# V weights in another pool, double-buffered keys, gates at urgent priority, and the fill split around the scores

## The chip, the cores and the metric

The kernel runs on one core of a Trainium2 chip. The metric is the device time of one execution in microseconds (us), as a median over runs. A profile is one execution of the same program, recorded by the hardware profiler.

## The reference, cut to what matters

One layer of a streaming encoder is applied to a prompt of 1024 tokens and to 64 further tokens of a running stream (1088 columns in all, model width 1024). One input projection of x feeds two branches:

```python
qa, ka, va, za, qkv_b, a_b, b_b, z_b, g_a, g_b = in_projection(x, w_in)
# A: 16 query heads on 4 key heads of 64, chunks of 64 see their own and two chunks before, a sink in the softmax
qa, ka = partial_rope(qa), partial_rope(ka)
oa  = window_attention(qa, ka, va, attn_sinks)
y_a = (oa * silu(za)) @ w_o_attn
# B: causal convolution, SiLU, normalised q and k, a delta rule in chunks of 64 with decays from a_b, b_b
y_b = (rmsnorm(delta(silu(conv(qkv_b)), gates(a_b, b_b))) * silu(z_b)) @ w_o_delta
h   = sigmoid(g_a) * y_a + sigmoid(g_b) * y_b
y   = layer_norm(ALPHA * x + h @ w_out)
```

Outputs are y, the new keys and values of the window, the last rows before the convolution, and the delta states.

## The kernel before, in words

Tile writes the semaphores. Each instruction has a priority, and a list scheduler with a model of the times decides, before the run, the order of the instructions on every engine and in the DMA queue of SyncE (SP). On the chip each engine then takes its instructions strictly in that order. `urgent()` gives what it encloses the highest priority. Matmuls are kept in the order in which the program traces them (`mm`, L108), transposes too (`tr`, L111), and a `split` with `pin=True` stays behind the ScalarE instruction traced before it.

Every product in full precision is three matmuls: both operands are split into a high and a low part by `split` (L88 on ScalarE, L91 on VectorE), and high*high, high*low and low*high are summed in PSUM. PSUM has eight banks here: three under the tag `pj` (`pjt()`) and five under `bg` (`ps()`).

The program goes through these stages:

1. `load_x` loads and splits x. `branch_a_keys` projects the keys in six groups (three column groups, two pairs of heads). Each group is copied to SBUF (`rraw`), rotated with a shuffled copy (`rsh`), added, split by `key_parts` into `rsh` (high) and `klo` (low), and written to DRAM (`k_d`) by four DMAs for each call of `put`. All of these tiles have one buffer. The last column group calls `put` twice, and the cached keys add two more calls.
2. `vab` projects V and the decay inputs with weights of 272 columns (tile `wt`, both parts and all eight blocks, in pool `vb`). 24 matmuls make one of nine tiles.
3. `plain` weaves `gates` (decays of branch B; its scratch tile is one more tile of tag `klo`) with `early`, the first two tiles of z_A. `early` keeps its tanh results in the tags `rraw` and `rsh`. Two matmul groups of `gates` stand in the order of TensorE: one after the first 24 matmuls of `early`, one after the next 24. The sums of x for the next stage (`sums_x`, GpSimd) follow; their splits are pinned on ScalarE.
4. `front` and `stream` make queries, z_A and merge gates by a seven-product scheme on quarters. Weights come from `weights7` in the tags `whi`, `wlo` and `wx` (three buffers, pool `ws`). The evacuation of a gate is `land` (L407: PSUM plus a saved part into a tile `gs`, urgent), a tanh (L619) and for z_A a multiply (L621) into another `gs`, and a DMA. `gs` has five buffers.
5. `attention` goes through 36 units. Iteration i does `values` of unit i-3, `flip` (transposes the probabilities of unit i-2 into two `bg` banks, copied out by ScalarE and VectorE, L719), `scores` of unit i (eight matmuls into two `bg` banks, L686 to L701 behind them), and then yields `UNIT`. `weave` fills that yield with matmuls of the merge gates until 8797 columns are done. `values` holds two more `bg` banks over two units, until L763 reads them.
6. Branch B: four pairs of heads, projections woven with the delta rule. `pair_project`, `gate_project` and `zb_project` use tiles `gt` (three buffers).
7. `out_a`, `out_b`, `final`: output projections, also with `gt`, and the layer norm. `out_a` loads a stored merge gate into `gt` (L1123), multiplies it with PSUM (L1124), and stores it (L1125). Its first tile evacuates all three column groups at its end.

Of the kernel before, what the change touches and what calls it, by code (L numbers as in the profile page):

```python
# [25 lines left out]
KT = 8  # L26
# [22 lines left out]
UNIT = 8797  # L49
# [6 lines left out]
class Build:  # L56
# [180 lines left out]
    def consts(self):  # L237
        nc, I = self.nc, self.I
        cf = self.t(self.cp, [128, 2 * 128 + 2 * 64], "cf")
        nc.sync.dma_start(cf, I["cf"])  # L240
        c = lambda i: cf[:, i * 128 : (i + 1) * 128]
        self.ident, self.stru2 = c(0), c(1)
        self.later = self.t(self.cp, [128, 128], "later", F32R)
        nc.scalar.activation(self.later, self.stru2, AF.Copy)
        c = lambda i: cf[:, 256 + i * 64 : 256 + (i + 1) * 64]
        self.cmask, self.id64 = (c(i) for i in range(2))
        self.masks = self.t(self.cp, [128, 2, 32], "masks", U8)
        mf = self.t(self.vb, [128, 384], "rsh", bufs=1)[:, :64].rearrange("p (a b) -> p a b", a=2)
        nc.sync.dma_start(mf, I["masks"])
        nc.vector.tensor_copy(self.masks, mf)  # L250
        sm = self.t(self.cp, [128, 24 * 4 + 24 * 3 + 4 + 4 + 1 + 8 + 12], "sm")
        nc.sync.dma_start(sm, I["small"])
        self.convw = sm[:, 0:96].rearrange("p (t j) -> p t j", j=4)
        self.sconv = sm[:, 96:168].rearrange("p (t j) -> p t j", j=3)
        self.alog, self.dtb, self.dnw = sm[:, 168:172], sm[:, 172:176], sm[:, 176:177]
        self.sink = sm[:, 177:185].rearrange("p (g u) -> p g u", u=2)
        self.m4, self.m16, self.m32, self.m64 = sm[:, 185:189], sm[:, 189:191], sm[:, 191:195], sm[:, 195:197]
        self.nsink = self.t(self.cp, [128, 4, 2], "nsink")
        nc.vector.tensor_scalar(self.nsink, self.sink, -1.0, None, ALU.mult)
        self.ncv = self.t(self.cp, [128, 24, 2, 3], "ncv")  # L260
        self.cg = []
        for i in range(2):
            c = self.t(self.ws, [128, HN], "u", bufs=6)[:, :256]
            nc.sync.dma_start(c, I["cg"][:, i * 256 : i * 256 + 256])
            self.cg += [c[:, :128], c[:, 128:]]
# [143 lines left out]

    def vab(self):  # L410
        nc, I = self.nc, self.I
        wt = self.t(self.vb, [128, 2, KT, 272], "wt", F32R)
        hi, lo = wt[:, 0], wt[:, 1]
        for k in (0, 4):
            wr = self.t(self.wp, [128, 4, 272], "wraw", bufs=2)
            with self.urgent():
                nc.sync.dma_start(wr, I["w_vab"][k : k + 4].rearrange("k p c -> p k c"))
                self.split(hi[:, k : k + 4], lo[:, k : k + 4], wr)
        self.V = self.t(self.ap, [128, 9, 256], "V")
        abt = self.t(self.ap, [128, 9, 16], "abt")  # L420
        with self.urgent():
            rest = self.rest(self.t(self.wp, [128, KT, 128], "whi", F32R, bufs=2), self.ring)
        nc.vector.memset(abt, 0.0)
        for t in range(9):
            m = 128 if t < 8 else 64
            ps = self.pjt()
            o = ps[:m, :272]
            for kt in range(KT):
                if t < 8:
                    xh, xl = (self.ring[kt][:, s, t * 128 : t * 128 + m] for s in (0, 1))  # L430
                    self.mm(o, xh, hi[:, kt], kt == 0, False)
                    self.mm(o, xl, hi[:, kt], False, False)
                    self.mm(o, xh, lo[:, kt], False, kt == KT - 1)
                else:
                    self.mm(ps[:, :272], rest[:, kt], hi[:, kt], kt == 0, False)
                    self.mm(ps[:, :272], rest[:, kt], lo[:, kt], False, kt == KT - 1)
            with self.urgent():
                nc.scalar.activation(self.V[:m, t, :], ps[:m, :256], AF.Copy)
                nc.scalar.activation(abt[:m, t, :], ps[:m, 256:272], AF.Copy)
        with self.urgent():  # L440
            for dst, c in ((self.V, slice(0, 256)), (abt, slice(256, 272))):
                nc.vector.tensor_tensor(dst[:m, 8, :], ps[64:128, c], dst[:m, 8, :], ALU.add)
        return abt
# [13 lines left out]
    def early(self):  # L457
        nc = self.nc
        for t in range(2):
            def ev(g, a, n, ps):  # L460
                th = self.t(self.vb, [128, 384], ("rraw", "rsh")[g % 2], bufs=1)[:, :n]
                nc.scalar.activation(th, ps, AF.Tanh, scale=0.5)
                nc.vector.scalar_tensor_tensor(th, th, 1.0, ps, ALU.add, ALU.mult)
                nc.sync.dma_start(self.zA[t, :, a : a + n], th)

            yield from self.project(ev, soon=True)


    def gates(self, abt):
# [3 lines left out]
        sw = self.ps()  # L473
        self.mm(sw[:, :144], swap, abt.rearrange("p t c -> p (t c)"))
        sw = sw[:, :144].rearrange("p (t c) -> p t c", c=16)
        scr = self.t(self.vb, [128, 384], "klo", bufs=1)
        gb = scr[:, 0:144].rearrange("p (t c) -> p t c", c=8)
        g4 = gb.rearrange("p (t two) c -> p t two c", two=2)
        nc.vector.tensor_copy(g4[0:64, :, 0, :], abt[0:64, :, 0:8])
# [51 lines left out]
    def branch_a_keys(self):  # L531
        nc, I = self.nc, self.I
        self.load_rope(self.vb, "rope")


        def put(gp, src, dst):
            n = src.shape[-1]
            for s, part in enumerate(self.key_parts(src)):
                for hf in range(2):
                    nc.sync.dma_start(self.k_d[gp, :, 2 * s + hf, dst : dst + n], part[HS[hf]].bitcast(F32))  # L540

        for g, (a, n) in enumerate(GROUPS):
            for gp in range(2):
                ps = self.ps()[:, :n]
                for kt in range(KT):
                    self.drain(self.mm3(ps, *self.w0[gp], kt, a, n, kt == 0, kt == KT - 1))
                raw, sh = (self.t(self.vb, [128, 384], x, bufs=1)[:, :n] for x in ("rraw", "rsh"))
                nc.scalar.activation(raw, ps, AF.Copy)
                self.rope(raw, sh, a, n, KSWAPMASK)
                nc.vector.tensor_tensor(raw, raw, sh, ALU.add)  # L550
                w = min(n, SEQ - a)
                put(gp, raw[:, :w], a)
                if g == 2:
                    put(gp, raw[:, w:], SEQ + 128)
                    nc.sync.dma_start(self.O["o_nkp"][:, gp], raw[:, w - 128 : w])
                    nc.sync.dma_start(self.O["o_nks"][:, gp, 64:128], raw[:, w:])
        ck = self.t(self.vb, [128, 384], "rraw", bufs=1)[:, :256].rearrange("p (g n) -> p g n", g=2)
        nc.sync.dma_start(ck, I["cache_k"])
        for gp in range(2):
            put(gp, ck[:, gp], SEQ)  # L560
        nc.sync.dma_start(self.O["o_nks"][:, :, 0:64], ck[:, :, 64:128])

    def key_parts(self, src):
        n = src.shape[-1]
        parts = [self.t(self.vb, [128, 384], x, F32R, bufs=1)[:, :n] for x in ("rsh", "klo")]
        self.split(*parts, src)
        return parts

# [9 lines left out]
    def front(self):  # L578
# [32 lines left out]
        def gate(dst, t, silu):  # L611
            def ev(m, a, ps, add):
# [2 lines left out]
                    src = self.t(self.gsp, [128, HN], "gs", bufs=5)  # L615
                    self.land(src, ps, add)
                th = self.t(self.gsp, [128, HN], "gs", bufs=5)
                with nullcontext() if src is not ps else self.urgent():
                    nc.scalar.activation(th, src, AF.Tanh, scale=0.5)  # L619
                    if silu:  # L620
                        nc.vector.scalar_tensor_tensor(th, th, 1.0, src, ALU.add, ALU.mult)  # L621
# [21 lines left out]
    def gate_project(self, tiles):  # L643
        nc = self.nc
        for i in tiles:
            dst = (self.gA, self.gB)[i // 8]

            def ev(g, a, n, ps):
                th = self.t(self.mp, [128, 384], "gt", bufs=3)
                nc.scalar.activation(th[:, :n], ps, AF.Tanh, scale=0.5)  # L650
                nc.sync.dma_start(dst[i % 8, :, a : a + n], th[:, :n])

# [90 lines left out]
    def attention(self):  # L743
# [6 lines left out]
        for i in range(len(units) + 3):  # L750
# [14 lines left out]
            if 1 < i <= len(units) + 1:  # L765
                unit = units[i - 2]
                PT[unit] = self.flip(unit[0], P.pop(unit))
            if i < len(units):
                P[units[i]] = self.scores(*units[i])
            yield UNIT  # L770


    def pair_project(self, p, qkv):
        nc = self.nc
        self.order = LATER if p == 0 else EARLY
        for s in range(3):
            for h in range(2):
# [3 lines left out]
                def ev(g, a, n, ps, s=s, h=h, ct=ct, prev=prev):  # L781
# [13 lines left out]
                        nc.gpsimd.tensor_copy(self.ncv[:, ct, 0, :], pre[:, 256:259])  # L795
                        nc.gpsimd.tensor_copy(self.ncv[:, ct, 1, :], pre[:, 323:326])
                    acc = self.t(self.bp, [128, 384], "acc", bufs=2)
                    th = self.t(self.mp, [128, 384], "gt", bufs=3)
                    cw = lambda j: self.convw[:, ct, j : j + 1]
                    nc.scalar.activation(acc[:, :w], pre[:, 0:w], AF.Copy, scale=cw(0))  # L800
                    for j in range(1, 4):
# [15 lines left out]
    def zb_project(self, p):  # L817
        nc = self.nc
        for h in range(2):
            def ev(g, a, n, ps):  # L820
                th = self.t(self.mp, [128, 384], "gt", bufs=3)
                nc.scalar.activation(th[:, :n], ps, AF.Tanh, scale=0.5)
                nc.vector.scalar_tensor_tensor(th[:, :n], th[:, :n], 1.0, ps, ALU.add, ALU.mult)  # L823
                nc.sync.dma_start(self.zsd[2 * p + h, :, a : a + n], th[:, :n])
# [293 lines left out]
    def out_a(self, w):  # L1118
        nc = self.nc
        for t in range(8):  # L1120
            def ev(g, a, n, ps):
                tg = self.t(self.mp, [128, 384], "gt", bufs=3)
                nc.sync.dma_start(tg[:, :n], self.gA[t, :, a : a + n])  # L1123
                nc.vector.scalar_tensor_tensor(tg[:, :n], tg[:, :n], 1.0, ps, ALU.add, ALU.mult)  # L1124
                nc.sync.dma_start(self.hA[t, :, a : a + n], tg[:, :n])  # L1125
# [2 lines left out]
    def out_b(self, w):  # L1128
# [2 lines left out]
        self.wo = self.t(self.pl, [128, KT, D], "pl", F32R), self.t(self.fp, [128, KT, D], "wolo", F32R)  # L1131
        for t in range(8):
            def ev(g, a, n, ps):
                tg = self.t(self.mp, [128, 384], "gt", bufs=3)
                ha = self.t(self.fp, [128, 384], "ha", bufs=2)
                nc.sync.dma_start(ha[:, :n], self.hA[t, :, a : a + n])
                nc.sync.dma_start(tg[:, :n], self.gB[t, :, a : a + n])
# [301 lines left out]
```

## Time and profile before

| | |
|---|---|
| runs, median (range) | 1448.79 us (1445.99 to 1452.46), 3 runs |
| profiled execution, device time | 1446.86 us |
| its span | 1445.1 us, 30842 instructions |
| TensorE matmul busy | 1375.4 us (95%) |
| TensorE weight load busy | 1280.2 us (89%) |
| VectorE busy | 988.8 us (68%) |
| ScalarE busy | 626.6 us (43%) |
| GpSimd busy | 228.8 us (16%) |
| mean granted clock of TensorE | 0.981 |

The span goes from the first to the last instruction of the profile; the device time has a little around it. PE is the matmul part of TensorE and PEld its weight loads; DVE is VectorE, ACT ScalarE, POOL GpSimd and SP SyncE, whose queue issues nearly all DMAs. "idle before" is time in which an engine had nothing running, and the releaser is what ended it. In a timeline a row gives the start, the length, the line, the operation, the tile written and the tiles read, and in brackets the idle time before it with its releaser. A tile's name is that of its tag, so the scratch tile of `gates` appears as klo.

### The profile page before, as it was taken

The numbers are of one execution on the slowest core, as the hardware profiler recorded it, in microseconds if no ns is written. First come the engines' busy times: TensorE is split into PE (matmuls) and PEld (weight loads), VectorE is DVE, ScalarE is ACT, GpSimd is POOL, SyncE is SP. The second block draws the span as 40 slices with busy tenths as digits, with TensorE's granted clock in tenths as the row PEclk, the third lists the DMA queues.
The fourth block names the chain that finished last, engine by engine and source line by source line (L and its number), as shares of the span: only waits on it lengthen the run. The fifth ranks groups of instructions, "written<-read, shape, count | busy, mean of one in ns | idle before, by whom it ended". The sixth has DMA issues, their size and how long they took to land. (4 is left out here: it accounts for less than half of the span.)

```text
span 1445.1 us, 30842 instructions
## 1 busy us (share of the span) xinstructions
PE 1375.4 (95%) x11850; PEld 1280.2 (89%) x11850; DVE 988.8 (68%) x2404; ACT 626.6 (43%) x1764; POOL 228.8 (16%) x373
## 2 busy tenths in 40 slices
PE   8839999989999999999999999999998999999997
PEld 8839999978888999998899888988898889999886
DVE  7447755656777747977778677867879555654676
ACT  5234444445545535436652565345644344322100
POOL 5114322210011101311130111211130100000000
PEclk9969999999999999999999999999999999999999
DMA  7312576566655541020122102211156224574221
GB/s 262 89 43 75 152 161 166 162 180 165 162 162 153 158 128 45 30 76 16 42 90 88 36 31 66 89 56 46 50 182 199 91 76 141 186 236 153 92 88 73
DMA packets 153013, 162.47 MB, mean 112 GB/s; under 512 B 54305, under 2 KB 136609, under 8 KB 152481
## 3 DMA queue, kind: packets, MB, share of 16 engines
q1 hardware_dynamic: 139664, 150.26, 34.9%
q10 hardware_dynamic: 13200, 10.23, 2.3%
q8 instruction: 94, 1.54, 0.5%
q14 instruction: 55, 0.44, 0.1%
HBM read 111.74 MB, written 48.70 MB: 111 GB/s over the span
## 5 line engine op out<-in xcount | busy, mean ns | idle before, releaser
L108 PE MATMUL pj<-ring,whi 128*128 128x384 f32 (+2 forms) x2856 | 678.5, 328 | 4.2 <-DVE gt L1124 4.2
L108 PEld LDWEIGHTS pj<-ring,whi 128*128 128x128 f32 x2856 | 482.4, 190 | 15.0 <-issue 13.7
L108 PE MATMUL pj<-ring,wlo 128*128 128x384 f32 (+2 forms) x1680 | 464.9, 321 | 0.2
L108 PEld LDWEIGHTS pj<-ring,wlo 128*128 128x128 f32 x1680 | 288.9, 189 | 4.9 <-issue 4.0
L802 DVE SCALAR_TENSOR_TENSOR acc<-pre,sm,acc 128x384 f32<-128x384 f32 (+1 forms) x216 | 134.0, 627 | 26.3 <-ACT acc L800 22.9
L108 PE MATMUL pj<-ring,wx 128*128 128x272 f32 x756 | 109.4, 294 | 10.5 <-DVE gs L407 5.6
L108 PEld LDWEIGHTS pj<-ring,wx 128*128 128x128 f32 x756 | 101.3, 193 | 12.1 <-DVE gs L407 5.8
L88 ACT ACTIVATE whi<-wraw 128x1024 fp32r<-128x1024 f32 (+2 forms) x72 | 66.7, 927 | 79.3 <-PE pj L108 42.6
L91 DVE TENSOR_TENSOR wlo<-wraw,whi 128x1024 fp32r<-128x1024 f32 (+2 forms) x58 | 66.7, 1150 | 38.8 <-ACT whi L88 34.0
L108 PE MATMUL bg<-ring,whi 128*128 128x384 f32 (+2 forms) x408 | 84.7, 318 | 4.3 <-ACT ring L88 4.3
L695 ACT ACTIVATE P<-bg,nm 128x192 f32<-128x192 f32 (+2 forms) x136 | 54.7, 410 | 47.3 <-DVE nm L688 46.1
L108 PEld LDWEIGHTS bg<-ring,whi 128*128 128x128 f32 x408 | 66.1, 192 | 5.8 <-ACT ring L88 4.8
L108 PE MATMUL pj<-pl,ring 128*128 128x512 f32 (+1 forms) x240 | 70.1, 375 | 0.0
L1014 DVE SCALAR_TENSOR_TENSOR S<-S,dec,bg 128x128 f32<-128x128 f32 x128 | 38.7, 344 | 39.1 <-PE bg L108 38.2
L108 PE MATMUL bg<-ring,wlo 128*128 128x272 f32 (+2 forms) x288 | 63.7, 308 | 0.0
L803 ACT ACTIVATE gt<-acc 128x384 f32<-128x384 f32 (+1 forms) x72 | 36.4, 505 | 62.5 <-DVE acc L802 62.2
L992 ACT ACTIVATE qs<-bg,egs 64x128 f32<-64x128 f32 x128 | 46.4, 362 | 29.4 <-DVE R L989 27.6
L330 POOL TENSOR_TENSOR sums<-wraw 128x512 f32<-128x512 f32 x14 | 19.0, 1357 | 243.5 <-DMA wraw<-w_tiles 181.8
L989 DVE SCALAR_TENSOR_TENSOR R<-bg,negc,t2k 64x128 f32<-64x128 f32 x128 | 44.6, 349 | 16.3 <-PE bg L108 15.1
L809 DVE SCALAR_TENSOR_TENSOR plb<-gt,acc 128x384 f32<-128x384 f32 (+1 forms) x96 | 43.1, 461 | 15.6 <-ACT gt L803 15.3
L108 PEld LDWEIGHTS pj<-pl,ring 128*128 128x128 f32 x240 | 44.1, 188 | 8.1
L108 PE MATMUL bg<-keys,q 128*128 128x192 f32 (+2 forms) x272 | 44.2, 289 | 7.3 <-ACT PT L719 3.0
(270 smaller groups left out, 2304.5 us busy)
## 6 DMA issues: line engine op xcount, KB each, us to landing
wraw<-w_tiles SPq DMA_DIRECT2D x80, 512.0 KB, 3.9
q_d<-qsp SPq DMA_DIRECT2D x32, 256.0 KB, 3.5
keys<-k_d SPq DMA_DIRECT2D x28, 256.0 KB, 4.2
q<-q_d SPq DMA_DIRECT2D x64, 96.0 KB, 3.0
gA_d<-gs SPq DMA_DIRECT2D x32, 136.0 KB, 2.6
plb<-prodA SPq DMA_DIRECT2D x8, 544.0 KB, 4.5
plb<-prodB SPq DMA_DIRECT2D x8, 544.0 KB, 4.8
z<-zA_d SPq DMA_DIRECT2D x16, 256.0 KB, 3.1
```

The costliest lines, as they stand in the source:

```text
L88: i = self.nc.scalar.activation(hi, raw, AF.Copy)
L91: self.nc.vector.tensor_tensor(lo, raw, hi.bitcast(F32), ALU.subtract)
L108: self.tc.keep_in_program_order(self.nc.tensor.matmul(o, l, r, start=start, stop=stop, skip_group_check=skip))
L330: sub = lambda d, x, y, op: nc.gpsimd.tensor_tensor(d, x, y, op)
L695: nc.scalar.activation(P[:, hf, k], ps[:, k], AF.Exp, bias=nm[:, hf, b : b + 1], scale=0.125, accum_out=sm[:, hf, b : b + 1])
L802: nc.vector.scalar_tensor_tensor(acc[:, :w], pre[:, j : j + w], cw(j), acc[:, :w], ALU.mult, ALU.add)
L803: nc.scalar.activation(th[:, :w], acc[:, :w], AF.Tanh, scale=0.5)
L809: nc.vector.scalar_tensor_tensor(o, v(th), 1.0, v(acc), ALU.add, ALU.mult)
L989: nc.vector.scalar_tensor_tensor(R[HS[h]], ks[HS[h], col[h]], self.negc[HS[h], p, c : c + 1], e["vs"][HS[h], i], ALU.mult, ALU.add)
L992: nc.scalar.activation(qs[HS[1 - h]], ks[HS[1 - h], col[h]], AF.Copy, scale=self.egs[HS[1 - h], p, c : c + 1])
L1014: nc.vector.scalar_tensor_tensor(Sn[:, h], S[:, h], self.egl[h][:, p, c : c + 1], kv[:, 0:128], ALU.mult, ALU.add)
```

## The change

Five edits:

- The weights of `vab` leave the tile `wt`. Each half of the blocks has a high and a low tile of 4 blocks; three of the four use the tag `wx` of pool `ws`, the last a smaller `wt`.
- `rraw`, `rsh` and `klo` get two buffers, the high part of the keys gets a tag of its own (`khi`, two buffers), and the scratch of `gates` gets a tile of its own (`scr`).
- In `front`, tanh and multiply of a gate are always traced as urgent, not only where they read PSUM directly.
- `gt` has four buffers, not three.
- In `attention`, half a `UNIT` is yielded between `flip` and `scores` and half after `scores`; the first two iterations yield a whole one after `scores`, the last three at most a half.

```diff
@@ consts, early, branch_a_keys: the tags rraw and rsh
-        mf = self.t(self.vb, [128, 384], "rsh", bufs=1)[:, :64].rearrange("p (a b) -> p a b", a=2)
+        mf = self.t(self.vb, [128, 384], "rsh", bufs=2)[:, :64].rearrange("p (a b) -> p a b", a=2)
...
@@ vab
-        wt = self.t(self.vb, [128, 2, KT, 272], "wt", F32R)
-        hi, lo = wt[:, 0], wt[:, 1]
+        wt = []
         for k in (0, 4):
             wr = self.t(self.wp, [128, 4, 272], "wraw", bufs=2)
+            parts = [self.t(pool, [128, 4, 272], tag, F32R, bufs=b)
+                     for pool, tag, b in (((self.ws, "wx", 3), (self.ws, "wx", 3)) if k == 0 else ((self.ws, "wx", 3), (self.vb, "wt", 1)))]
             with self.urgent():
                 nc.sync.dma_start(wr, I["w_vab"][k : k + 4].rearrange("k p c -> p k c"))
-                self.split(hi[:, k : k + 4], lo[:, k : k + 4], wr)
+                self.split(*parts, wr)
+            wt.append(parts)
+        hi, lo = ([wt[kt // 4][s][:, kt % 4] for kt in range(KT)] for s in range(2))
...
@@ gates
-        scr = self.t(self.vb, [128, 384], "klo", bufs=1)
+        scr = self.t(self.vb, [128, 384], "scr")
...
@@ branch_a_keys
-                raw, sh = (self.t(self.vb, [128, 384], x, bufs=1)[:, :n] for x in ("rraw", "rsh"))
+                raw, sh = (self.t(self.vb, [128, 384], x, bufs=2)[:, :n] for x in ("rraw", "rsh"))
...
@@ key_parts
-        parts = [self.t(self.vb, [128, 384], x, F32R, bufs=1)[:, :n] for x in ("rsh", "klo")]
+        parts = [self.t(self.vb, [128, 384], x, F32R, bufs=2)[:, :n] for x in ("khi", "klo")]
...
@@ front, gate
-                with nullcontext() if src is not ps else self.urgent():
+                with self.urgent():
                     nc.scalar.activation(th, src, AF.Tanh, scale=0.5)
...
@@ gate_project, pair_project, zb_project, out_a, out_b
-                th = self.t(self.mp, [128, 384], "gt", bufs=3)
+                th = self.t(self.mp, [128, 384], "gt", bufs=4)
...
@@ attention
                 PT[unit] = self.flip(unit[0], P.pop(unit))
+                yield UNIT * 0.5
             if i < len(units):
                 P[units[i]] = self.scores(*units[i])
-            yield UNIT
+                yield UNIT * (1.0 if i < 2 else 0.5)
```

More of the change, by code (lines that the diff above doesn't have):

```diff
@@ L430, in vab @@
                     xh, xl = (self.ring[kt][:, s, t * 128 : t * 128 + m] for s in (0, 1))
-                    self.mm(o, xh, hi[:, kt], kt == 0, False)
-                    self.mm(o, xl, hi[:, kt], False, False)
-                    self.mm(o, xh, lo[:, kt], False, kt == KT - 1)
-                else:
-                    self.mm(ps[:, :272], rest[:, kt], hi[:, kt], kt == 0, False)
-                    self.mm(ps[:, :272], rest[:, kt], lo[:, kt], False, kt == KT - 1)
+                    self.mm(o, xh, hi[kt], kt == 0, False)
+                    self.mm(o, xl, hi[kt], False, False)
+                    self.mm(o, xh, lo[kt], False, kt == KT - 1)
+                else:
+                    self.mm(ps[:, :272], rest[:, kt], hi[kt], kt == 0, False)
+                    self.mm(ps[:, :272], rest[:, kt], lo[kt], False, kt == KT - 1)
             with self.urgent():
@@ L460, in ev @@
             def ev(g, a, n, ps):
-                th = self.t(self.vb, [128, 384], ("rraw", "rsh")[g % 2], bufs=1)[:, :n]
+                th = self.t(self.vb, [128, 384], ("rraw", "rsh")[g % 2], bufs=2)[:, :n]
                 nc.scalar.activation(th, ps, AF.Tanh, scale=0.5)
@@ L556, in branch_a_keys @@
                     nc.sync.dma_start(self.O["o_nks"][:, gp, 64:128], raw[:, w:])
-        ck = self.t(self.vb, [128, 384], "rraw", bufs=1)[:, :256].rearrange("p (g n) -> p g n", g=2)
+        ck = self.t(self.vb, [128, 384], "rraw", bufs=2)[:, :256].rearrange("p (g n) -> p g n", g=2)
         nc.sync.dma_start(ck, I["cache_k"])
@@ L797, in ev @@
                     acc = self.t(self.bp, [128, 384], "acc", bufs=2)
-                    th = self.t(self.mp, [128, 384], "gt", bufs=3)
+                    th = self.t(self.mp, [128, 384], "gt", bufs=4)
                     cw = lambda j: self.convw[:, ct, j : j + 1]
@@ L820, in ev @@
             def ev(g, a, n, ps):
-                th = self.t(self.mp, [128, 384], "gt", bufs=3)
+                th = self.t(self.mp, [128, 384], "gt", bufs=4)
                 nc.scalar.activation(th[:, :n], ps, AF.Tanh, scale=0.5)
@@ L1121, in ev @@
             def ev(g, a, n, ps):
-                tg = self.t(self.mp, [128, 384], "gt", bufs=3)
+                tg = self.t(self.mp, [128, 384], "gt", bufs=4)
                 nc.sync.dma_start(tg[:, :n], self.gA[t, :, a : a + n])
@@ L1133, in ev @@
             def ev(g, a, n, ps):
-                tg = self.t(self.mp, [128, 384], "gt", bufs=3)
+                tg = self.t(self.mp, [128, 384], "gt", bufs=4)
                 ha = self.t(self.fp, [128, 384], "ha", bufs=2)
```

## The prediction

> **What bounds the kernel now.** I read the page first (busy shares, slices), then the waits of TensorE, then the timelines around each of its long waits, engine by engine. PE is busy for 1375.4 of 1445.1 us, so at most 69.7 us of idle time can be removed without touching the matmuls, and whatever PE is kept waiting for is path: its instructions run in one fixed order.
>
> ```profile
> span 1445.1 us, 30842 instructions
> PE 1375.4 (95%) x11850; PEld 1280.2 (89%) x11850; DVE 988.8 (68%) x2404; ACT 626.6 (43%) x1764; POOL 228.8 (16%) x373
> ...
> PE bg L108 <- DVE klo L495: 28.7, 1, 28.7
> PE pj L108 <- DVE gs L407: 5.6, 1, 5.6
> PE bg L108 <- ACT ring L88: 4.3, 1, 4.3
> PE pj L108 <- DVE gt L1124: 4.2, 1, 4.2
> PE bg L108 <- ACT PT L719: 3.0, 2, 2.7
> PE bg L108 <- DVE z L763: 2.9, 3, 1.4
> ```
>
> In the waits, the columns are total, count and longest. One wait of 28.7 us is two fifths of all idle time. The change touches four of PE's waits: this one, gs, gt, and those of the scores in the attention. It doesn't touch the 4.3 us at the start, where x is still arriving.
>
> **Part 1: keys, scratch and V weights.** The 28.7 us are the second matmul group of the gates waiting for the scratch tile (klo at L495). The fence shows TensorE, first around this wait and then around a later one, then DVE, then SP's queue.
>
> ```profile
> 61.94 0.41 PE L108 MATMUL bg<-abt,u 128*128 128x144 f32 x2
> 95.20 0.70 PE L108 MATMUL bg<-klo,u 128*128 128x68 f32 x2 [28.67 <-DVE klo L495]
> ...
> 293.66 3.09 PE L108 MATMUL pj<-ring,wx 128*128 128x272 f32 x12 [5.58 <-DVE gs L407]
> 296.55 2.08 PE L108 MATMUL pj<-ring,wlo 128*128 128x272 f32 x12
> ...
> 304.00 1.68 PE L108 MATMUL pj<-ring,wlo 128*128 128x272 f32 x12
> 305.51 0.66 PE L108 MATMUL pj<-ring,whi 128*128 128x272 f32 x4
> 306.10 0.81 PE L108 MATMUL bg<-PT,V 128*64 128x128 f32 x8
> ...
> 39.00 0.01 DVE L522 LOAD_MASK_SELECT rsh<-rraw  x1 [2.46 <-DMA k_d<-rsh]
> 41.86 0.56 DVE L91 TENSOR_TENSOR klo<-rraw,rsh 128x384 fp32r<-128x384 f32 x1 [0.59 <-ACT rsh L88]
> 44.68 0.01 DVE L522 LOAD_MASK_SELECT rsh<-rraw  x1 [2.26 <-DMA k_d<-rsh]
> 88.49 0.19 DVE L479 COPY klo<-abt 64x72 f32<-64x72 f32 x1 [0.21 <-DMA k_d<-klo]
> 93.78 1.37 DVE L495 TENSOR_TENSOR klo<-klo 128x68 f32<-128x68 f32 x1
> ...
> 35.85 1.14 SPq L540 DMA_DIRECT2D k_d<-rsh  x2
> 37.09 1.19 SPq L540 DMA_DIRECT2D k_d<-klo  x2
> 85.99 1.10 SPq L540 DMA_DIRECT2D k_d<-klo  x2
> ```
>
> The first gates matmul ran at 61.94; its result could have been read then, but L479, the first write of the scratch, starts at 88.49, released by a store of the keys. So the wait is a buffer: the scratch shares klo with the keys, whose chain has one buffer. A group goes from shuffle to shuffle in 44.68 - 39.00 = 5.68 us, of which DVE works from 39.00 to 42.42 and then waits 2.26 us for the store. With two buffers, DVE's own 3.4 us a group is the next bound, and then SP: a `put` is 1.14 + 1.19 = 2.33 us of issue, and ten of them (six groups, two second parts, two for the cache) make 23.3 us. From 35.85 that ends at 59.2 if SP is never late, and a few us later with its other DMAs; today the last store is issued at 85.99. With a scratch of its own, `gates` needs no store at all, only its place in DVE's order, and that is then around the end of the keys.
>
> From L479 to the matmul took 95.20 - 88.49 = 6.7 us. If it starts at 62.4, behind the first gates matmul, it ends at 69.1; PE arrives at 95.20 - 28.67 = 66.5. So 2.6 us of the stall stay, and I take 3 for keys still ahead in DVE's or ACT's order. Removed: 28.7 - 3 = 25.7. After a long wait PE also runs slowly: the 12 matmuls behind the 5.58 us wait take 296.55 - 293.66 = 2.89 us, a dozen alike later 305.51 - 304.00 = 1.51, so 1.4 us more. This goes too, if what stays is short: 27 us together. Bounds: 30 if the gates arrive in time, 17 if some 13 us of the key chain still stand before them.
>
> The V weights: same splits, same shapes, another address.
>
> ```profile
> 69.45 0.63 ACT L88 ACTIVATE wx<-sums 128x512 fp32r<-128x512 f32 x1 [5.91 <-POOL sums L330]
> ```
>
> This costs nothing, because the first other split into `wx` comes at 69.45, behind sums of weights, and V's matmuls all stand before the one of 61.94. If that cover went, the third product of the first job would wait, which has the following stall anyway.
>
> What is late next is the third product's operand from `sums_x`:
>
> ```profile
> 122.83 0.39 PE L108 MATMUL pj<-ring,wx 128*128 128x272 f32 x1 [1.96 <-ACT ring L88]
> 124.13 0.82 PE L108 MATMUL pj<-ring,wx 128*128 128x272 f32 x2 [0.92 <-DVE ring L91]
> 124.75 2.92 PE L108 MATMUL bg<-ring,wx 128*128 128x272 f32 x12
> ```
>
> PE waits 1.96 and 0.92 us, and the next 12 matmuls take 2.92 us. The splits behind this are pinned behind the tanhs of `early`, so they move up with PE; these 2.9 us and the slow stretch stay where they are relative to PE. If POOL doesn't keep pace, up to 2 us come on top; I take 0.
>
> **Part 2: gates urgent.**
>
> ```profile
> 292.70 0.43 ACT L619 ACTIVATE gs<-gs 128x272 f32<-128x272 f32 x1 [1.81 <-DMA zA_d<-gs]
> ...
> 287.68 2.89 SPq L676 DMA_DIRECT2D q<-q_d  x6
> 290.62 1.90 SPq L622 DMA_DIRECT2D zA_d<-gs  x4
> ```
>
> PE waits 5.58 us for L407, which needs a free `gs`. ACT's tanh waits for a z_A store; the store was issued at 290.62, behind six loads of q. With the tanh and multiply urgent in the planning, a `gs` pair is finished right behind `land` and its store is ready earlier. But the store itself stays at the low priority, in the same SP queue, and SP may still be held up in front of it. Cost of the wait now: 5.58 and the slow dozen's 1.4, 7.0 together. What urgency costs: each tanh (0.43 us by the row of 292.70) may go in front of an exponential; with part 3 there is fill to cover that. Bounds: -2 (the wait moves and exponentials come late) and 7; I take 4, because the queue that made it late is only half addressed.
>
> **Part 3: half a unit between flip and scores.**
>
> ```profile
> L108 PEld LDWEIGHTS bg<-keys,q 128*128 128x128 f32 x272 | 35.2, 191 | 11.4 <-ACT PT L719 7.2 <-DVE z L763 3.6 <-ACT PT L722 0.5
> ...
> 342.78 1.45 PE L108 MATMUL bg<-keys,q 128*128 128x192 f32 x8
> ...
> 402.32 0.91 PE L108 MATMUL bg<-keys,q 128*128 128x192 f32 x6 [2.71 <-ACT PT L719]
> 404.77 4.04 PE L108 MATMUL pj<-ring,wx 128*128 128x272 f32 x24
> ...
> 347.04 0.44 ACT L695 ACTIVATE P<-bg,nm 128x192 f32<-128x192 f32 x1
> ```
>
> The first row groups all weight loads of the scores: 11.4 us idle ahead of them, of which 7.2 wait for PT copies and 3.6 for z. The scores follow the transposes directly, with two banks in `values`, two in `flip` and two wanted, of five. In between there will now be some 16 matmuls of fill, 16 x 1.51/12 = 2.0 us, longer than a PT copy takes to start and finish in most units. One wait of 2.71 us is also followed by 24 matmuls in about 4.0 us instead of 3.0: 1 us more.
>
> Costs: an additional switch from fill to small matmuls per unit. Four fill matmuls before `values` take 306.10 - 305.51 = 0.59 (rows in part 1) instead of 4 x 1.51/12 = 0.50, so 0.09 x 34 = 3.1 us. Then the new wait: the second transpose needs a bank from the previous scores, now only half a fill back. It asks about 1.0 (scores) + 2.0 (fill) + 1.0 (values) + 0.3 (first transposes) = 4.3 us after the scores start. In a unit started at 342.78 the last exponential ends at 347.04 + 0.44 = 347.5, 4.7 us after; but the first bank is free two exponentials earlier, about 1.1 us, so 3.6. Margin 0.7 us: it is late only now and then. I take 2 us for this and for rests. Gain: 11.4 + 1 - 3.1 - 2 = 7.3; some of the 11.4 is the plain switch, which no order removes, so I take 6.5. Bounds: 12 (no new wait) and -3 (half a microsecond more in each unit). The scores' loads of q and keys move behind the half fill as the matmuls do and keep their priority, and the flip reads a unit's probabilities two iterations later, so nothing else becomes late. Two units less of fill are woven; the same matmuls run behind the attention, cost zero.
>
> [...]
>
> **Part 4: four `gt`.**
>
> ```profile
> 1116.34 0.71 PE L108 MATMUL pj<-ring,whi 128*128 128x384 f32 x2 [4.17 <-DVE gt L1124]
> 1120.04 0.54 PE L108 MATMUL pj<-ring,whi 128*128 128x384 f32 x2
> ...
> 1115.65 1.41 DVE L1124 SCALAR_TENSOR_TENSOR gt<-gt,pj 128x384 f32<-128x384 f32 x3
> ...
> 1104.80 1.32 SPq L824 DMA_DIRECT2D zs_d<-gt  x3
> 1109.35 1.27 SPq L1123 DMA_DIRECT2D gt<-gA_d  x3
> ```
>
> `out_a` stops PE for 4.17 us, and the 12 matmuls behind it (1116.34 to 1120.04) take 3.7 us where the dozen of 272 columns gives 1.51 x 384/272 = 2.1 us. The loads of the stored gates were issued at 1109.35, when the stores of 1104.80 had freed `gt`. In the planning the evacuation was therefore late, and DVE's order has a piece of the delta rule's block inversion in front of L1124. The fourth buffer lets the first of three loads go before those stores, and one free bank is enough for PE to go on: the next group of 24 takes 4.3 us, twice the 2.1. About 1 us of latency stays. Gain: 4.17 - 1 + 1.6 = 4.8 if DVE's order follows, 0 if not, -1 if something else shifts; I take 3.
>
> **Sum.** 27 + 4 + 6.5 + 3 = 40.5 us. The profiled execution took 1446.86 (span 1445.1), so 1406.4. The median of the runs shown is 1.9 above it, so 1408 for a median.
>
> [...]
>
> **The rivals.**
>
> A. The key chain gets faster, but its rest still stands before the gates, in the fixed orders of DVE and ACT, or behind SP. For it: 23.3 us of issue and SP's other DMAs. Against: the scratch needs none of them. Some 13 us of the stall stay: 27 becomes 17, so 1408 + 10 = 1418.
>
> B. Part 1 as forecast, and the rest nets nothing, because fixed orders that are planned anew put a wait elsewhere. For it: a store's place in SP's queue made the gs wait, not its priority. Time 1448.8 - 27 = 1422.
>
> C. All four hit fully: 30 + 7 + 12 + 4.8 = 53.8, so 1395.
>
> D. Slower: in the attention the transposes wait for the banks of the scores. Price: 34 units times the wait. The other parts give 34 us, so it decides from 1.0 us a unit (no change), that is, exponentials about 1.7 us later than in the row above; at 1.3 us a unit it costs 44 us, and the time is 1459. Against it: the margin of 0.7 and the second bank, which is also free before the next scores.
>
> E. Part 1 doesn't act: the gates stay in DVE's order behind the last keys and these keep their pace. Then parts 2 to 4 give some 5 us, about 1444. Against it: both buffers of the chain are doubled.
>
> **How the numbers follow.** Chances: the forecast (1400 to 1413) 0.45, A 0.17, B 0.18, C 0.12, E 0.04, D 0.04. The range takes the forecast with A and B, with A's bound of 17 and little from the rest (1426), and goes down into C to 1396: 0.45 + 0.17 + 0.18 + half of 0.12, about 0.86. A measurement of this kernel tells about 0.5%, 7 us, from no change. Faster by more: forecast, A, B, C and what E and D leave there, 0.94; within: most of E, 0.03; slower: most of D, 0.03.
>
> **What will show it.** Right: the wait for klo or scr at the gates' second group is under 5 us; keys' shuffles are 3.4 us apart, not 5.7; the gs wait near the attention's start is under 2; the weight loads of the scores wait under 4 us in all, those of the transposes no more than now; the wait at L1124 is near 1. Wrong: a key store or split just before L479 in DVE's order, a wait of the transposes for L695, or a `gs` wait that has only moved along.

## The result, and the profile after

The changed kernel takes 1414.07 us (median of 4 runs, 1412.57 to 1415.87), the kernel before 1450.62 beside it; the ratio is 0.9753 [0.9724, 0.9782], some 36 us. The prediction was 1408 (1396 to 1426). The profiled execution of before (1446.86) lies at the low end of its runs, so the two traces differ by 34.3 us in span (1445.1 to 1410.8). First the page and the waits of TensorE after the change:

```profile
span 1410.8 us, 30874 instructions
PE 1368.5 (97%) x11850; PEld 1275.8 (90%) x11850; DVE 978.4 (69%) x2404; ACT 623.5 (44%) x1764; POOL 227.9 (16%) x373
...
PE pj L108 <- ACT u L359: 6.0, 3, 3.5
PE bg L108 <- ACT ring L88: 4.8, 2, 4.5
PE bg L108 <- ACT abt L442: 4.5, 1, 4.5
PE pj L108 <- ACT ring L88: 3.8, 1, 3.8
PE pj L108 <- DVE gt L1128: 3.8, 1, 3.8
PE pj L108 <- DVE rraw L466: 1.5, 1, 1.5
```

The waits for klo (28.7), gs (5.6), PT (3.0) and z at the scores (2.9) are gone. The one for gt is nearly as it was (4.2 before). New are abt, 4.5, and rraw, 1.5. Ring in `pj` has grown from 1.96 to 3.8, and u from 2.0 to 6.0 in all; before, its row was

```profile
PE pj L108 <- ACT u L359: 2.0, 3, 1.2
```

TensorE's timeline after the change has them in the front part (the last u, 2.02 us at 145.95, stands behind these rows):

```profile
68.82 0.82 PE L108 MATMUL bg<-abt,u 128*128 128x144 f32 x2 [4.54 <-ACT abt L442]
75.29 0.33 PE L108 MATMUL bg<-scr,u 128*128 128x68 f32 x2
...
93.21 1.77 PE L108 MATMUL pj<-ring,whi 128*128 128x272 f32 x12 [1.51 <-DVE rraw L466]
103.05 1.80 PE L108 MATMUL pj<-ring,wx 128*128 128x272 f32 x9 [3.54 <-ACT u L359]
108.67 0.59 PE L108 MATMUL pj<-ring,wx 128*128 128x272 f32 x1 [3.82 <-ACT ring L88]
109.98 0.82 PE L108 MATMUL pj<-ring,wx 128*128 128x272 f32 x2 [0.71 <-DVE ring L91]
110.60 2.92 PE L108 MATMUL bg<-ring,wx 128*128 128x272 f32 x12
```

To see where time came and went I cut both traces at starts of matmuls that occur in every kernel: the first matmul of `gates`, its second group, the first scores, and the first matmul of branch B; the last stretch goes to the end of the last matmul. Each row is one profiled execution. The last four rows are experiments below.

| us between these | start to gates | to 2nd group | to first scores | attention | branch B to end |
|---|---|---|---|---|---|
| before | 61.9 | 33.3 | 167.5 | 268.9 | 904.6 |
| after | 68.8 | 6.5 | 173.2 | 248.1 | 905.4 |
| gain | -6.9 | 26.8 | -5.7 | 20.9 | -0.8 |
| half fill alone | 62.7 | 35.5 | 169.7 | 247.9 | 903.9 |
| unpinned | 81.2 | 6.1 | 159.2 | 248.9 | 904.9 |
| cached keys, rope first | 64.6 | 4.4 | 174.6 | 249.4 | 904.9 |
| sums early | 67.6 | 6.0 | 160.7 | 247.8 | 905.9 |

The stall itself gave 26.8 us, but 12.6 went back, 6.9 ahead of it and 5.7 behind it, so the front nets 14.2 where 27 was forecast for part 1. The attention gave 20.9, where parts 2 and 3 had 10.5 together.

**What took the 12.6 us back.** First before (DVE, then SP's queue), then after (DVE, SP's queue, ACT, POOL):

```profile
13.96 8.23 DVE L91 TENSOR_TENSOR ring<-ring,ring 128x384 fp32r<-128x384 f32 x16
32.23 0.68 DVE L523 TENSOR_TENSOR rraw<-rraw,cs 128x384 f32<-128x384 f32 x1 [0.87 <-DMA cs<-rope]
...
26.30 0.43 SPq L528 DMA_DIRECT2D cs<-rope  x1
```

```profile
14.57 14.29 DVE L91 TENSOR_TENSOR ring<-ring,ring 128x384 fp32r<-128x384 f32 x16
38.20 0.56 DVE L526 TENSOR_TENSOR rraw<-rraw,cs 128x384 f32<-128x384 f32 x1 [4.71 <-DMA cs<-rope]
...
31.62 0.43 SPq L531 DMA_DIRECT2D cs<-rope  x1
65.15 0.43 SPq L561 DMA_DIRECT2D rraw<-cache_k  x1
71.82 0.54 SPq L324 DMA_DIRECT2D wraw<-w_tiles  x1
...
67.33 0.51 ACT L88 ACTIVATE khi<-rraw 128x128 fp32r<-128x128 f32 x2 [8.86 <-DMA rraw<-cache_k]
78.80 0.63 ACT L88 ACTIVATE wx<-sums 128x512 fp32r<-128x512 f32 x1 [5.11 <-POOL sums L330]
81.27 0.49 ACT L465 ACTIVATE rsh<-pj 128x384 f32<-128x384 f32 x1
82.08 1.21 ACT L88 ACTIVATE ring<-ring 128x544 fp32r<-128x544 f32 x2
...
76.07 1.30 POOL L330 TENSOR_TENSOR sums<-wraw 128x512 f32<-128x512 f32 x1 [41.95 <-DMA wraw<-w_tiles]
```

Three things are to be seen. The last sixteen of DVE's splits of x take 14.29 us instead of 8.23. V's splits are late with them, and so is the rope table (asked for at 31.62 instead of 26.30, behind a load of weights whose buffer V's split frees), for which the keys wait on DVE. Then ACT waits 8.86 us for the cached keys, which SP asks for behind nearly all stores of the keys; the last evacuation of V stands behind that, and the gates with it (4.54). Last, ACT waits 5.11 us for POOL's sums of weights, whose load was late in the same queue, and `early`'s tanh (L465) and the pinned splits of the sums of x stand behind that: TensorE's waits from 93 to 110 us. Each is tried below.

### The profile page after: what moved, and what is told of

Its sections match the earlier page's. It is cut to its first block, busy times and chain, and to the rows that moved or that the text cites. A ratio compares the mean times of both kernels' runs of the same rounds, so it can differ in the third digit from the quotient of the medians.

```text
span 1410.8 us, 30874 instructions
## 1 busy us (share of the span) xinstructions
PE 1368.5 (97%) x11850; PEld 1275.8 (90%) x11850; DVE 978.4 (69%) x2404; ACT 623.5 (44%) x1764; POOL 227.9 (16%) x373
## 5 line engine op out<-in xcount | busy, mean ns | idle before, releaser
L698 ACT ACTIVATE P<-bg,nm 128x192 f32<-128x192 f32 (+2 forms) x136 | 54.4, 408 | 33.2 <-DVE nm L691 30.3
L804 ACT ACTIVATE acc<-pre,sm 128x384 f32<-128x384 f32 (+1 forms) x72 | 42.8, 597 | 15.7 <-DVE plb L813 6.1
```

The costliest lines, as they stand in the source:

```text
L698: nc.scalar.activation(P[:, hf, k], ps[:, k], AF.Exp, bias=nm[:, hf, b : b + 1], scale=0.125, accum_out=sm[:, hf, b : b + 1])
```

## The experiments

Unless said otherwise, a run differs from the changed kernel or the kernel before by the lines shown; long edits are shown in part. Each ratio is against the kernel before as it ran beside that run, and the interval behind it is one of 95%.

**One part at a time, on the kernel before.** Part 1 alone (V's weights, buffers of the keys, `scr`):

> The kernel before with part 1 alone (V weights in wx, keys in two buffers, scratch of its own). Theory 1, from the two traces: part 1 nets 14 us and not 27, because the cached keys stand ahead of V's last evacuation in ScalarE's order and wait for a load that SP issues behind the key stores; so ratio 0.990, some 1434 us, with a wait of TensorE for abt of about 4.5 us. Rival: part 1 alone brings the 27 us of the forecast (ratio 0.981, 1422 us), and the other parts take some of it away again.

Measured 1432.35, ratio 0.9869 [0.9849, 0.9889], about 19 us (16 to 22): between the two, with neither 14 nor 27 in the interval. (The profiled executions differ by 13.3 us, but that of before is a quick one.) The gs wait is still 5.6, and the wait for abt is 4.2. Half the fill alone (the two `yield` lines of the attention):

> The kernel before with half a unit of fill between flip and scores alone. Theory 1: the waits inside the scores were larger than their idle rows show; 13 us go (ratio 0.991), and the gs wait of 5.6 us near the attention's start stays. The forecast's step: 6.5 us (0.9955). Rival: the gs wait goes with this edit alone, 20 us together (0.986).

Measured 1429.57, ratio 0.9841 [0.9814, 0.9868], about 23 us: the largest part, and it takes the gs wait with it, as the rival has it. The longest wait left is that of part 1:

```profile
PE bg L108 <- DVE klo L495: 30.9, 1, 30.9
```

The urgent tanhs alone (`with self.urgent():`):

> The kernel before with urgent gates alone. Theory 1: the gs wait of 5.6 us and the slow stretch behind it go, 7 to 8 us (ratio 0.995). The forecast's step: 4 us (0.997). Rival: it is the half fill that removed the wait, and this edit alone gives nothing (1.000).

Measured 1451.9, ratio 1.0 [0.9987, 1.0013]. Its SP queue, then that of half the fill alone:

```profile
292.68 2.91 SPq L676 DMA_DIRECT2D q<-q_d  x6
295.64 1.90 SPq L622 DMA_DIRECT2D zA_d<-gs  x4
```

```profile
279.85 5.11 SPq L676 DMA_DIRECT2D q<-q_d  x8
285.01 1.41 SPq L622 DMA_DIRECT2D zA_d<-gs  x3
287.67 0.52 SPq L574 DMA_DIRECT2D keys<-k_d  x1
```

Urgency leaves the four stores behind the six loads of q, as before the change (287.68 and 290.62), and the wait of 5.6 us with them. With fill between flip and scores the planner puts three of these stores in front of the next loads. Four `gt` alone (`bufs=4`):

> The kernel before with four gt buffers alone. Theory 1: nothing (ratio 1.000), because L1124 stands at the same place in VectorE's order, whenever its load lands; the wait of TensorE for gt stays near 4 us. The forecast's step: 3 us (0.998).

Measured 1451.85, ratio 1.0007 [0.999, 1.0024]. So of four parts two work; for the other two the intervals allow some 2 us.

**The two that work, without the others** (`gt` with three buffers, the old rule for urgent):

> The changed kernel without its urgent gates and without the fourth gt: part 1 and the half fill alone. Theory 1: these two are the whole change; ratio 0.975 as with all parts (1414 us), no gs wait over 1 us. Rival: together with the half fill urgency matters after all, and the ratio is 0.980 or more.

Measured 1411.66, ratio 0.973 [0.9712, 0.9749]: all of the gain, its interval overlapping that of the whole change. The two parts alone multiply to 0.9869 x 0.9841 = 0.9712, the lower end of this interval, so no interaction is seen.

**What in part 1 works.** The changed kernel with one buffer for each of the keys' tiles (and for `early`'s results, which have the same tags); `scr`, the tag `khi` and V's weights as changed:

```diff
-    raw, sh = (self.t(self.vb, [128, 384], x, bufs=2)[:, :n] for x in ("rraw", "rsh"))
+    raw, sh = (self.t(self.vb, [128, 384], x, bufs=1)[:, :n] for x in ("rraw", "rsh"))
...
-    parts = [self.t(self.vb, [128, 384], x, F32R, bufs=2)[:, :n] for x in ("khi", "klo")]
+    parts = [self.t(self.vb, [128, 384], x, F32R, bufs=1)[:, :n] for x in ("khi", "klo")]
```

> The changed kernel with one buffer for each tile of the keys again, the scratch of the gates still a tile of its own. Theory 2: the scratch alone doesn't help, since the keys at their old pace then stand in ScalarE's order before V's last evacuation and the first gates matmul; the long wait moves from the second gates matmul to the first (for abt), and the ratio is 0.985 or more. Rival: the scratch was all that mattered: the ratio stays at 0.975.

Measured 1413.6, ratio 0.9744 [0.9728, 0.9761]: the same time.

```profile
PE pj L108 <- ACT ring L88: 10.8, 1, 10.8
...
PE bg L108 <- ACT abt L442: 3.6, 1, 3.6
...
PE bg L108 <- DVE scr L498: 2.9, 1, 2.9
```

The gates wait 2.9 us for the scratch, though the keys have one buffer and their last low parts are stored as late as in the kernel before (at 84.70 us; 85.99 there). So what removed the 28.7 us is the scratch's own tile. The double buffers bring nothing that reaches the end: in this run the wait for ring is 10.8 us instead of 3.8, but the gates' groups come at 65.8 and 73.4 us, earlier than in the changed kernel (68.8 and 75.3).

**The front: cached keys and rope tables.** The lines that load and split the cached keys stand ahead of the six groups:

```diff
+        ck = self.t(self.vb, [128, 384], "rraw", bufs=2)[:, :256].rearrange("p (g n) -> p g n", g=2)
+        nc.sync.dma_start(ck, I["cache_k"])
+        for gp in range(2):
+            put(gp, ck[:, gp], SEQ)
...
         for g, (a, n) in enumerate(GROUPS):
```

> The changed kernel with the cached keys taken first, ahead of the six projected groups. Theory 2: what stayed of the stall and what followed it (TensorE's waits for abt, 4.5 us, for L466, 1.5, and 2 to 4 us more in the third product of the first job) comes from the cached keys' split, which waits 8.9 us in ScalarE's queue for its load behind SP's stores; with it gone, 8 us fewer than the changed kernel: ratio 0.970, 1406 us. Rival: SP's 23 us of issue for key stores is the bound wherever the cached keys stand: not over 2 us from the changed kernel.

Measured 1411.27, ratio 0.9729 [0.9712, 0.9745]: nearly nothing. ACT then waits 13.06 us for the cached keys, up to 38.94, with the keys' other splits behind it. With the rope tables' load right behind that of x as well, urgent:

> As cache_first, and the rotation tables are loaded right behind x, not behind the weights that wait for a buffer. Theory 3: the tables landed 6 us late in the changed kernel (VectorE idles 4.7 us for them), so the key chain starts some 5 us earlier, and the stall at the gates is gone: another 2 to 4 us, ratio 0.968. Rival: the tables take bandwidth from x at the start, TensorE's first matmuls come later, and it is no better than cache_first.

Measured 1408.75, ratio 0.9707 [0.9687, 0.9727], 5 us below the changed kernel by the medians, with intervals that just touch. The gates come 4.2 us earlier (table) and their wait for abt is down to 0.6, but the chain behind them stays:

```profile
64.64 0.41 PE L108 MATMUL bg<-abt,u 128*128 128x144 f32 x2
...
88.29 2.50 PE L108 MATMUL pj<-ring,whi 128*128 128x272 f32 x12 [2.78 <-DVE rraw L466]
98.11 1.49 PE L108 MATMUL pj<-ring,wx 128*128 128x272 f32 x9 [2.00 <-ACT u L359]
103.73 0.59 PE L108 MATMUL pj<-ring,wx 128*128 128x272 f32 x1 [4.13 <-ACT ring L88]
```

**The sums of x.** The changed kernel without the pin:

```diff
-                self.split(d[:, 0], d[:, 1], x, True)
+                self.split(d[:, 0], d[:, 1], x)
```

> The changed kernel, with the twelve splits of the sums of x no longer pinned behind the instruction traced before them on ScalarE. The planner then places most of them between the keys' splits. Theory 1: what took back the rest of the 28.7 us is this chain: on ScalarE the pinned splits stand behind the first weight split into wx, which waits 5.11 us for GpSimd's sums, and TensorE then waits 1.5 (L466), 3.5 (u), 3.8 and 0.7 us (ring) between 92 and 111 us. Unpinned, these go, all but 1 or 2 us: 6 to 9 us less than the changed kernel's 1414, so 1405 to 1408, and the first scores start at 240 to 243 instead of 248.5. Theory 2: the waits are only where the front is late, and VectorE, which now does twelve more splits before the keys' chain is through (some 8 us of work), brings the gates later by as much: within 3 us of the changed kernel, with the wait moved to abt or scr.

Measured 1410.15, ratio 0.971 [0.969, 0.973], some 4 us below the changed kernel by the medians, with intervals that overlap. Both theories hold in part: the stretch from the second gates group to the scores shrinks from 173.2 to 159.2 us, and the start grows from 68.8 to 81.2, because ACT now meets these splits before POOL has the sums:

```profile
27.82 1.21 ACT L88 ACTIVATE ring<-ring 128x544 fp32r<-128x544 f32 x2 [6.09 <-POOL ring L271]
38.08 0.66 ACT L88 ACTIVATE ring<-ring 128x544 fp32r<-128x544 f32 x1 [6.30 <-POOL ring L271]
```

**DVE and POOL.** POOL is made to wait for V's last low part (`self.late`), in front of its first sum of x:

```diff
+            if k == 0:
+                self.nc.gpsimd.tensor_copy(t3[:, 0, 0:1], self.late)
             sub(t3, b22, b12)
```

> The changed kernel, with one element copied by GpSimd ahead of its first difference of x; it reads the last low part of V's weights, so GpSimd's differences begin behind VectorE's splits of x. The copy's element is overwritten. Theory 1: in the changed kernel VectorE's sixteen splits of x take 14.29 us instead of 8.23, because from 19.06 us on GpSimd's and VectorE's two-input instructions take turns, 1.6 us each; without GpSimd VectorE keeps 0.55 to 0.48 us each, the sixteen take 8 us, V's splits and the rope tables' loads come 5 us earlier, and part of it, 2 to 5 us, reaches the end: 1409 to 1412. Theory 2: the sums are now later, and the front is bound by them and ScalarE's queue: VectorE's splits speed up in the same way, and the end doesn't move, 1414, or is 1 to 3 us later.

Measured 1410.38, ratio 0.9717 [0.9699, 0.9735], 3.7 us below the changed kernel by the medians, with intervals that overlap. The edit only half acts: the planner puts four differences that don't touch `t3` in front of the copy, and for these DVE and POOL still take turns. When POOL stops, DVE's splits are at once at 0.48 us again. All sixteen end at 26.2 instead of 28.9 us:

```profile
14.07 3.36 DVE L91 TENSOR_TENSOR ring<-ring,ring 128x384 fp32r<-128x384 f32 x7
17.73 8.48 DVE L91 TENSOR_TENSOR ring<-ring,ring 128x384 fp32r<-128x384 f32 x9 [0.29 <-ACT ring L88]
```

**The banks in the attention.** The changed kernel with all of the fill between flip and scores:

```diff
-                yield UNIT * 0.5
+                yield UNIT
             if i < len(units):
                 P[units[i]] = self.scores(*units[i])
-                yield UNIT * (1.0 if i < 2 else 0.5)
+                if i < 2:
+                    yield UNIT
```

> The changed kernel, with the whole unit of fill between flip and scores, none behind the scores. Theory 1: five banks are one too few for values, flip and scores, so whatever follows the scores without fill has to wait for their evacuation: scores wait for nothing, but the transposes come 1.0 (scores) + 1.0 (values) + 0.3 = 2.3 us after the scores' start, the first bank is free after about 3.6, so they wait up to 1.3 us in each of 34 units: 20 to 44 us more than the changed kernel, 1434 to 1458. Theory 2: only the wait of the scores behind the flip mattered, and the transposes find a bank anyway: 1414, within 4 us.

Measured 1434.23, ratio 0.9878 [0.9856, 0.99]: 20 us above the changed kernel by the medians, the lower end of the first theory. The weight loads of scores and of transposes (columns: busy us, mean ns, idle us ahead of them and its releasers), after the change and then in this run:

```profile
L108 PEld LDWEIGHTS bg<-keys,q 128*128 128x128 f32 x272 | 33.6, 191 | 0.0
L111 PEld LDWEIGHTS bg<-cf,P 128*128 128x128 f32 (+1 forms) x200 | 20.9, 138 | 9.4 <-issue 6.0 <-ACT P L698 2.1 <-DVE z L766 1.1
```

```profile
L108 PEld LDWEIGHTS bg<-keys,q 128*128 128x128 f32 x272 | 33.6, 191 | 0.0
L111 PEld LDWEIGHTS bg<-cf,P 128*128 128x128 f32 (+1 forms) x200 | 20.4, 139 | 31.0 <-ACT P L698 18.4 <-DVE z L766 6.5 <-DVE mx L689 3.6
```

The scores still wait for nothing, and the transposes, which now have only `values` and no fill between the scores and themselves, wait 31.0 - 9.4 = 21.6 us more, 0.6 us a unit, mostly for the exponentials that empty the scores' banks (L698). So the unit needs fill on both sides of the scores: without it ahead of them they wait for the banks of the transposes (7.2 us of their idle weight loads for PT before the change, 0.0 after), without it behind them the transposes wait for theirs (18.4 us of it for L698). Other shares than half and half were not tried.

**A version that beats both.** Part 1, half the fill, cached keys and rope tables first, without parts 2 and 4; and the sums of x for three of the four blocks traced within `vab`, so that their pinned splits stand between V's evacuations, where ACT waits little for POOL (0.86 and 2.85 us):

```diff
+        self.sums = self.sums_x()
...
                 nc.scalar.activation(abt[:m, t, :], ps[:m, 256:272], AF.Copy)
+            if t in (2, 4, 7):
+                next(self.sums), next(self.sums)
...
-        sums = self.sums_x()
+        sums = self.sums
...
-            for _ in range(18):
+            for _ in range(72):
```

> The parts that counted and no others: part 1, half the fill before the scores, cached keys and rope tables first (as in the run before this one that had them), gates not urgent beyond the old rule, three gt; and the sums of x for three of the four blocks are traced within vab, behind V's tiles 2, 4 and 7, so that their pinned splits stand between the evacuations of V instead of behind ScalarE's wait for the sums of weights. Theory 1: the waits that the run with rope tables first still had around the third product (2.8 at L466, 2.0 for u, 4.1 and 0.7 for ring, and a slow dozen of 1.4 behind them) are this chain; without them 6 to 10 us go from its 1408.75: 1399 to 1403, the best of all. Theory 2: the nine splits (9 times 0.55 us on ScalarE, 0.7 on VectorE) hold up the keys' chain or V's evacuations by as much, as the unpinned run showed with its 8.5 us for abt: 1406 to 1412.

Measured 1397.68, ratio 0.9628 [0.961, 0.9646]: 16 us below the changed kernel, and 11 below the run with the tables first, where 6 to 10 were expected. The third product runs without a wait, where 2.92 us had gone for a dozen:

```profile
95.97 1.66 PE L108 MATMUL pj<-ring,wx 128*128 128x272 f32 x12
97.46 1.66 PE L108 MATMUL bg<-ring,wx 128*128 128x272 f32 x12
```

The table shows the place: 160.7 us from the second gates group to the first scores, where the run with cached keys and tables first has 174.6 and the changed kernel 173.2. The gates come at 67.6 us, between these two (64.6 and 68.8). So the splits behind ACT's wait are worth some 13 us there. That is more than the 5.7 which the change gave back in this stretch: they held up the kernel before, too (167.5).

## Why the prediction was right, and where it was not

The time and the sign were right, but the sum was right by luck: two errors of opposite sign met.

| part | forecast (bounds) | alone, by its ratio |
|---|---|---|
| 1, keys and scratch | 27 (17 to 30) | 19 (16 to 22) |
| 2, urgent | 4 (-2 to 7) | 0 (-2 to 2) |
| 3, half fill | 6.5 (-3 to 12) | 23 (19 to 27) |
| 4, four gt | 3 (-1 to 4.8) | -1 (-3 to 1) |

- **Part 1.** The reading of the wait was right: it was a buffer, the gates needed only a place in DVE's order, and from the first gates matmul to the second group 26.8 us went where 25.7 were counted; there is no wait left at the second group. The step that failed is the next one: "If POOL doesn't keep pace, up to 2 us come on top; I take 0", and that the pinned splits keep their place relative to PE. PE came earlier, but ACT's pinned splits stand behind the weights' sums of POOL, and these behind SP's key stores: 5.7 us back between the gates and the scores. Nor had I looked ahead of the gates, where 6.9 us went back. Rival A had a rest of the key chain before the gates, and the cached keys are that; its 13 us were 4.5 at that place. The sign of being wrong that I had named came too: the cached keys' splits stand at 67.67 us in DVE's order, just before the first writes of the scratch from V's last tile (68.75). Four shuffles start at 42.81, 44.73, 47.67 and 50.09 us in the trace of after, 2.4 us apart on average, where I expected 3.4. That V's weights in their new place cost nothing was not tried alone. Against it stands that DVE's slow splits of x come with part 1: all ten runs that have it show them, the four others do not (last section). Its double buffers are not the cause, for the run with single ones shows them too; which of its other edits is, stays open.
- **Part 2** was worth 4 only if the stores moved. I wrote that they keep their low priority in SP's queue, and then took 4 against that; the run gave 0. In the changed kernel the wait is gone by part 3.
- **Part 3** was mis-sized in every term. Summed from start to start of neighbouring matmuls, scores to scores fell from 41.6 to 25.4 us (236 pairs). Of these 16.2 us, 2.9 have only moved: the first step behind the transposes is slow, a median of 172 ns where it is 88 behind fill, and now it falls to the fill (210 ns instead of 125). The other 13.3 stand against the 11.4 of idle weight loads, which leave out what a late load overlaps of the one before it (a load lasts 191 ns, and without a wait the next starts after some 111). The switch from fill to scores costs 125 ns, as from fill to fill (1.51/12 = 126), so the 3.1 us for it were 0; the 0.09 us belongs to the switch to `values` alone. The new wait at the transposes was there, 19.8 to 23.0 us from transpose to transpose, 3.2 instead of 2, and the idle time of their weight loads grew from 6.0 to 9.4, where I expected no more than before. Fill to fill and to scores fell from 161.6 to 153.7, although it took over the 2.9, so 10.8 us went there: some 8 of it at the gs wait and the slow stretch behind it, 1.5 behind the wait of 2.71 us, where I had counted 1. Without the gs wait this makes about 13, above my bound of 12.
- **Part 4.** The bound of 0 "if not" was right. In the trace of after, SP, then DVE, then PE:

```profile
1065.01 0.38 SPq L1127 DMA_DIRECT2D gt<-gA_d  x1
1073.94 0.81 SPq L1127 DMA_DIRECT2D gt<-gA_d  x2
...
1079.51 0.73 DVE L909 TENSOR_TENSOR t2k<-t2k,t2k 128x338 f32<-128x338 f32 x1
1080.15 1.40 DVE L1128 SCALAR_TENSOR_TENSOR gt<-gt,pj 128x384 f32<-128x384 f32 x3
...
1080.84 0.98 PE L108 MATMUL pj<-ring,whi 128*128 128x384 f32 x2 [3.78 <-DVE gt L1128]
```

The first load goes 15 us ahead of its evacuation (1080.15), where it was 6 before, as forecast. But all three evacuations keep their place in DVE's order, behind the block inversion (L909), and PE's wait stays.

- **Rivals.** B came nearest as a mechanism: fixed orders that are planned anew put a wait elsewhere, in the front. D is real, but at half the fill it is 3.2 us in all; with all of the fill before the scores it costs 0.6 us a unit. C and E did not occur.

## What to carry to other kernels

A long wait for a buffer is worth the wait minus what the same engines' queues hold next: before forecasting its removal, follow ACT, POOL and SP for as long again behind the wait and name the next late instruction. Where a matmul group needs banks that a group shortly before it still holds, share the other matmuls out among the gaps: half a unit on each side of the scores gained some 23 us, and all of it on one side lost 20 of them again. A priority helps only if it moves what ends the wait: here that was a store in SP's queue, and urgent gates left it where it was.

## What was not expected of the hardware

In both traces DVE's two-input splits of x take 0.48 to 0.56 us each as long as POOL is idle. Once POOL's two-input differences run, some instructions of the two take longer. In before POOL's first took 3.56 us and DVE kept its 0.48, until its last split took 1.44; after, from 19.06 us on, the two take turns, 1.56 to 1.63 us a difference and 1.65 to 1.67 a split, and sixteen splits take 14.29 us instead of 8.23. Two rows show the two cases, before and after:

```profile
18.27 6.47 POOL L271 TENSOR_TENSOR ring<-ring 128x544 f32<-128x544 f32 x3 [17.44 <-DMA ring<-xT]
```

```profile
19.06 3.15 POOL L271 TENSOR_TENSOR ring<-ring 128x544 f32<-128x544 f32 x2 [18.23 <-DVE ring L91]
```

So one of the two or both were slowed in each trace, and holding POOL back gave DVE its pace again (0.48 us). By what they are slowed is not shown. What DVE was doing when POOL's first difference began does not tell the two cases apart: in both a split was under way, begun at 18.11 us before and at 18.89 after.

What decides between these two cases is open. In the four runs without part 1 (before, half the fill alone, urgent alone, four `gt` alone) POOL's first difference takes 3.56 us; in the ten with part 1 it takes 1.55 to 1.95, and the two take turns from there on. What released POOL does not separate them: with four `gt` alone it was a split of DVE, with the cached keys first a DMA.

The slow dozens behind short waits of TensorE show in its granted clock. In before it is 0.50 from 124.7 to 127.7 us, behind waits of 1.96 and 0.92, and 0.74 from 402.3 to 408.8, behind the wait of 2.71. After, it is 0.50 from 110.6 to 113.5, behind waits of 3.82 and 0.71; in the last version, which doesn't wait there, it is 1.00 from 95 to 99, and the two dozens from 95.97 us take 1.66 us each.
